# Last layer's output projection as seven-product 2x2 block products, the merged tiles mixed pair by pair

## Chip, core and metric

The kernel runs on one core of one Trainium2 chip. The metric is the time of one execution on the device in microseconds (us), the median over repeated runs. A core has five engines with a queue each that runs in order: TensorE (PE, with its weight loads as PEld), VectorE (DVE), ScalarE (ACT), GpSimd (POOL) and SyncE (SP), which here only issues DMAs. PE's products are added up in PSUM, in tiles of 128x512 float32 (a bank each); DVE and ACT read them from there.

## What is computed

Two residual layers over x of 1024 positions by 1024 channels, float32. The edit touches the end of the second:

```
y_a = (o_a * silu(z_a)) @ w_attn_proj[l]          # 512 -> 1024 channels
y_f = (fourier(u_f) * silu(z_f)) @ w_fourier_proj[l]
m   = sigmoid(g_a + b_a) * y_a + sigmoid(g_f + b_f) * y_f
x   = x + m @ w_out[l]                            # 1024 x 1024 by 1024 x 1024
```

Attention, the Fourier branch, the norms and the input projection stay as they were.

## The kernel before

All activations are kept transposed: 128 channels on the partitions, 1024 positions along the free axis, so 1024 channels are eight tiles t = 0 to 7. A float32 product is made of three faster ones: each operand is split into hi, the value rounded to the shorter type fp32r, and lo, the rest. `mm3` (L162 to L167) adds hi x hi, hi x lo and lo x hi in PSUM, so a 128x128 block by 128x512 costs three matmuls of 128x512. The hi part of a split is a copy and the lo part a subtraction: `split_pool` (L129 to L132) does both on POOL, `split_fast` (L134 to L137) puts the copy on ACT and the subtraction on DVE, `wtile` (L139) loads a weight tile and splits it on POOL. Weight tiles live in the pool `wp`, which has two buffers each of raw, hi and lo. `stage` (L123) loads a 128x1024 tile into one of three buffers.

`merge` (L782) ends a layer. The attention output oG (four tiles) is split. Then for each of eight tiles t: load and sigmoid the gate (L801, L802), load the Fourier term mf, multiply the tile's weights by oG (24 matmuls, PSUM tile ya, two buffers), and on DVE multiply by the gate out of PSUM (L805) and add mf (L806), both 1024 wide; the result sa is the merged tile. It is split into mT, hi on ACT (L807) and lo on DVE (L808). After all eight, the output projection runs eight tiles xo of 8 K-tiles x 2 halves x 3 = 48 matmuls. The first runs its last K-tile last (`fm_late`), since mT's last tile comes late. DVE adds x to each finished xo (L821), and SP stores it (L822), the last tile in two halves. For the first layer, the same loop also feeds the next layer.

Memory pools lie on two sides of SBUF, which the layers swap: in the last layer mT is on the left with `wp` and `stage`, oG on the right; in layer 0 mT is on the right. What an engine does next is not the program's order alone: the tile framework's scheduler plans each queue when the kernel is built, by program order among what it expects to be ready, and adds the waits. At run time each queue then goes strictly in that planned order.

Of the kernel before, what the change touches and what calls it, by code (L numbers as in the profile page):

```python
# [33 lines left out]
F_ATT = (0, 0, 0, 0, 2, 0, 0, 0, 0, 0, 0, 0, 0, 0, 0, 1, 0, 1, 0, 0, 0, 1, 0, 0, 0, 1, 0, 0, 0, 1, 0, 0, 0, 1, 0, 0, 0, 0, 0, 0, 0, 1, 0, 0, 0, 1, 0, 0, 0, 1, 0, 0, 0, 0, 0, 0, 0, 1, 0, 0, 0, 0, 0, 1)  # L34
B_P, B_E, B_PT, B_KT, B_PF, B_S = (6, 8), 4, 4, 2, 2, 3
ORD = "SFVV"
SEQ = ('u z0 T F0 z1 C0 G0 F1 z2 C1 F2 G1 C2 F3 z3 M C3 G2 G3', 'u z0 T F0 z1 C0 G0 F1 z2 C1 F2 G1 C2 F3 z3 G2 M C3 G3')
U0, ZF0, GA0, GF0 = 4, 8, 12, 20


def f(ap):
    return ap.bitcast(F32)


class Trunk:
# [355 lines left out]
    def phase_a(self, l, xg, fp, gF):  # L401
# [330 lines left out]
    def attention(self, l, ap, sum_e):  # L732
# [7 lines left out]
        for i, (h, c) in enumerate(units):  # L740
            nxt = self.prep(l, *units[i + 1], ap, st) if i + 1 < len(units) else None
            for j in range(4):
                k = 2 * j
                for what in ORD:
                    if what == "S" and nxt:
# [33 lines left out]
            cur = nxt  # L779
        return za  # L780

    def merge(self, l, og3, x_ctx, res_d, out_d):  # L782
        tc, nc, io = self.tc, self.nc, self.io
        sub, mult, add = ALU.subtract, ALU.mult, ALU.add
        for _ in self.filler:
            pass
        self.psum(f"pm{l}")
        x_ctx.close()
        xs, os = self.xs, self.os
        m_ctx = ExitStack()  # L790
        mp = m_ctx.enter_context(tc.tile_pool(name=f"m{l}", bufs=1, side=xs))
        with tc.tile_pool(name=f"og{l}", bufs=1, side=os) as op_:
            oG = [op_.tile([P, 4, S], F32R, name=f"oG{j}") for j in range(2)]
            mT = [mp.tile([P, KD, S], F32R, name=f"mT{j}") for j in range(2)]
            for t in range(4):
                o = self.stage(self.og_d[t], f"og{t}") if t < 3 else og3
                nc.scalar.activation(oG[0][:, t, :], o, AF.Copy)
                nc.vector.tensor_tensor(oG[1][:, t, :], o, f(oG[0][:, t, :]), op=sub)
            for t in range(KD):
                sa = op_.tile([P, S], F32, tag="sa", bufs=2, name=f"sa{t}")  # L800
                nc.sync.dma_start(sa, self.ga_d[t])  # L801
                nc.scalar.activation(sa, sa, AF.Sigmoid, bias=self.bm[:, l, 0, t:t + 1])  # L802
                mf = self.stage(self.mf_d[t], f"mfl{t}")
                ps = self.fm(self.wtile(io["w_ap"][l, t], 4, f"wa{t}"), oG, 4, f"ya{t}")
                nc.vector.tensor_tensor(sa, ps, sa, op=mult)  # L805
                nc.vector.tensor_tensor(sa, sa, mf, op=add)  # L806
# [4 lines left out]
        if not last:  # L811
            xp = n_ctx.enter_context(tc.tile_pool(name=f"x{l + 1}", bufs=1, side=os))
            xg = [xp.tile([P, KD, S], F32R, name=f"xg{l + 1}{j}") for j in range(2)]
        with tc.tile_pool(name=f"xo{l}", bufs=1, side=xs) as op_:
            for t in range(KD):
                xr = self.stage(res_d[t], f"xr{t}")
                w = self.wtile(io["w_o"][l, t], KD, f"wo{t}")
                ps = self.fm_late(w, mT, f"xo{t}") if t == 0 else self.fm(w, mT, KD, f"xo{t}")
                dst = out_d[t] if last else self.x1_d[t]
                for cs in (slice(0, 512), slice(512, S)) if last and t == KD - 1 else (slice(0, S),):  # L820
                    nc.vector.tensor_tensor(xr[:, cs], ps[:, cs], xr[:, cs], op=add)  # L821
                    nc.sync.dma_start(dst[:, cs], xr[:, cs])  # L822
                if not last:
                    self.feed(l + 1, t, xr, op_, xg)
            if not last:
                self.norm(op_)
        m_ctx.close()
        return None if last else (xg, n_ctx)

    def run(self):  # L830
        tc, nc, io = self.tc, self.nc, self.io
        x_ctx = ExitStack()
        xp = x_ctx.enter_context(tc.tile_pool(name="x0", bufs=1, side="right"))
        xg = [xp.tile([P, KD, S], F32R, name=f"xg0{j}") for j in range(2)]
        raw = self.wp.tile([P, 1024], F32, tag="raw", name="wu0_r")
# [117 lines left out]
```

## Time and profile before

| what | value |
|---|---|
| median of 3 runs | 1682.37 us (1681.14 to 1683.57) |
| profiled execution | 1685.97 us, of which the span 1684.2 us |
| PE, PEld busy | 1651.1 us (98%), 1348.4 us (80%) |
| DVE, ACT, POOL busy | 833.5 us (49%), 635.8 us (38%), 727.9 us (43%) |
| last merge: ya stage, xo stage | 1547.6 to 1592.4 us, 1592.4 to 1679.5 us |

The span runs from the first to the last instruction of the program; the profiled execution's own time has some 2 us around it. Busy time of an engine is time in which an instruction of it runs; for an engine that waited inside an instruction, for a shared resource, that time counts as busy too. Matmuls overlap in the record, so PE's pace is read from the distance of their starts or from a stretch divided by their number, not from the duration of one (some 390 ns here).

### The profile page before, as it was taken

Reading aid. Unit: us, or ns where it says so; the run is one execution under the profiler, and the core shown is the slowest. Engines: PE = TensorE matmul, PEld = TensorE weight load, DVE = VectorE, ACT = ScalarE, POOL = GpSimd, SP = SyncE. Lnnn points to the kernel's source line nnn. Section 1 sums busy time; section 2 is a strip of 40 time slices with the busy share of each in tenths; the row PEclk is TensorE's granted clock in tenths of the full one; section 3 lists DMA queues with packets and bytes.
Section 4 is the critical chain, followed back from the end, with each engine's and each line's share of the span. In section 5 each row is a group of like instructions: output and inputs, shape, how many; then the busy total and the mean of one; then the engine's idle time right before and its main releaser. Section 6 shows DMA issues by size and latency. Waiting matters only on the chain.

```text
span 1684.2 us, 22506 instructions
## 1 busy us (share of the span) xinstructions
PE 1651.1 (98%) x8374; PEld 1348.4 (80%) x8374; DVE 833.5 (49%) x1358; ACT 635.8 (38%) x1233; POOL 727.9 (43%) x567
## 2 busy tenths in 40 slices
PE   7999999999999999999999999999999999999998
PEld 5888889887777877777888888888877777777887
DVE  7643452332666666565324435424246666664711
ACT  4322321312666666522112223213147666663300
POOL 5622361474453543443254324524643545543531
PEclk9999999999999999999999999999999999999999
DMA  5302230343555553474342023213454555534741
GB/s 193 131 13 70 90 125 32 126 181 131 191 183 184 179 186 143 156 241 158 126 144 75 13 77 115 106 50 129 173 172 165 192 176 188 192 143 163 239 148 76
DMA packets 118366, 234.76 MB, mean 139 GB/s; under 512 B 27888, under 2 KB 48624, under 8 KB 118000
## 3 DMA queue, kind: packets, MB, share of 16 engines
q1 hardware_dynamic: 117904, 228.59, 39.4%
q0 software_dynamic: 352, 4.73, 0.7%
q8 instruction: 66, 1.08, 0.3%
q14 instruction: 44, 0.36, 0.1%
HBM read 116.89 MB, written 49.28 MB: 99 GB/s over the span
## 4 chain that ended last, share of the span: by engine, by line
PE 86%; DMA 4%; DVE 3%; ACT 3%; issue 2%; POOL 1%; SPq 0%; DVEq 0%; ACTq 0%; POOLq 0%
PE pt L714 4%; PE s L165 4%; PE o L718 4%; PE o L720 3%; PE s L167 3%; PE s L166 3%; PE gf L167 3%; PE gf L166 3%; PE gf L165 3%; PE xo L166 3%; PE xo L167 3%; PE xo L165 3%; PE ga L165 3%; PE ga L167 3%; PE ga L166 3%; DMA P<-E 2%
## 5 line engine op out<-in xcount | busy, mean ns | idle before, releaser
L693 DVE TENSOR_REDUCE nm<-s 128x1 f32<-128x512 f32 x256 | 173.0, 687 | 110.4 <-PE s L167 109.0
L700 ACT ACTIVATE E<-s,nm 128x512 f32<-128x512 f32 x256 | 173.3, 684 | 57.5 <-issue 28.6
L714 PEld LDWEIGHTS pt<-identr,P 128*128 128x128 f32 x1024 | 114.4, 141 | 43.0 <-DMA P<-E 7.4
L131 POOL TENSOR_SCALAR pT<-pf 128x512 fp32r<-128x512 f32 x96 | 59.4, 619 | 188.4 <-ACT pf L725 167.6
L132 POOL TENSOR_TENSOR pT<-pf,pT 128x512 fp32r<-128x512 f32 x96 | 123.7, 1289 | 8.0
L714 PE MATMUL pt<-identr,P 128*128 128x128 f32 x1024 | 121.7, 239 | 5.5 <-DMA P<-E 5.5
L196 DVE TENSOR_TENSOR pT<-pt,pT 128x512 fp32r<-128x512 f32 x160 | 109.3, 685 | 28.8 <-ACT pT L195 27.0
L165 PE MATMUL s<-kT,qT 96*128 96x512 f32 x256 | 110.8, 433 | 3.6 <-ACT E L700 2.4
L195 ACT ACTIVATE pT<-pt 128x512 fp32r<-128x512 f32 x160 | 95.7, 598 | 44.5 <-PE pt L714 44.5
L718 PE MATMUL o<-pT,V 128*128 128x512 f32 x256 | 109.7, 429 | 0.0
L720 PE MATMUL o<-pT,V 128*128 128x512 f32 x256 | 106.9, 418 | 0.0
L165 PE MATMUL ga<-xg,wga_h 128*128 128x512 f32 x256 | 103.4, 404 | 0.0
L167 PE MATMUL ga<-xg,wga_l 128*128 128x512 f32 x256 | 102.7, 401 | 0.0
L166 PE MATMUL ga<-xg,wga_h 128*128 128x512 f32 x256 | 102.2, 399 | 0.0
L165 PE MATMUL gf<-xg,wgf_h 128*128 128x512 f32 x256 | 101.0, 395 | 0.0
L166 PE MATMUL s<-kT,qT 96*128 96x512 f32 x256 | 100.9, 394 | 0.0
L167 PE MATMUL gf<-xg,wgf_l 128*128 128x512 f32 x256 | 100.9, 394 | 0.0
L166 PE MATMUL gf<-xg,wgf_h 128*128 128x512 f32 x256 | 100.9, 394 | 0.0
L167 PE MATMUL s<-kT,qT 96*128 96x512 f32 x256 | 97.4, 397 | 0.0
L165 PE MATMUL xo<-mT,wo_h 128*128 128x512 f32 x224 | 87.9, 392 | 0.0
L166 PE MATMUL xo<-mT,wo_h 128*128 128x512 f32 x224 | 87.9, 392 | 0.0
L167 PE MATMUL xo<-mT,wo_l 128*128 128x512 f32 x224 | 87.9, 392 | 0.0
(334 smaller groups left out, 4221.3 us busy)
## 6 DMA issues: line engine op xcount, KB each, us to landing
P<-E SPq DMA_DIRECT2D x256, 256.0 KB, 2.3
kv_d<-KV SPq DMA_DIRECT2D x16, 640.0 KB, 2.9
KVh<-kv_d SPq DMA_DIRECT2D x16, 640.0 KB, 4.6
wgf_r<-in_w_fm SPq DMA_DIRECT2D x16, 512.0 KB, 3.5
mf_d<-sgf SPq DMA_DIRECT2D x16, 512.0 KB, 3.3
wga_r<-in_w_fm SPq DMA_DIRECT2D x16, 512.0 KB, 3.6
ga_d<-sga SPq DMA_DIRECT2D x16, 512.0 KB, 2.7
sa<-ga_d SPq DMA_DIRECT2D x16, 512.0 KB, 3.8
```

The source lines that it names most:

```text
L131: nc.gpsimd.tensor_scalar(hi, src, 1.0, 1.0, op0=ALU.mult, op1=ALU.mult)
L132: nc.gpsimd.tensor_tensor(lo, src, f(hi), op=ALU.subtract)
L165: self.nc.tensor.matmul(out, ah, bh, start=(i == 0), stop=False)
L166: self.nc.tensor.matmul(out, ah, bl, start=False, stop=False)
L167: self.nc.tensor.matmul(out, al, bh, start=False, stop=(i == n - 1))
L195: nc.scalar.activation(hi, ps, AF.Copy)
L196: nc.vector.tensor_tensor(lo, ps, f(hi), op=ALU.subtract)
L693: nc.vector.tensor_reduce(nm2[:, kc:kc + 1], s_ps, axis=AX.X, op=ALU.max)
L700: nc.scalar.activation(e, halves[kc], AF.Exp, bias=nm, accum_out=sum_e[:, h, t, kc:kc + 1])
L714: nc.tensor.transpose(tp[:, j * P:(j + 1) * P].bitcast(F32R), u["P"][j][k // 4][:, (k % 4) * P:(k % 4 + 1) * P], self.identr)
L718: nc.tensor.matmul(u["o"], u["V"][:, kk, :], q[0], start=(u["n"] == 0), stop=False)
L720: nc.tensor.matmul(u["o"], u["V"][:, kk, :], q[1], start=False, stop=(u["n"] == ST))
```

## The change

The first layer keeps `merge`. The last one has a `merge_last` of its own. Its output product is done on blocks: for output tiles 2j and 2j + 1 (j = 0 to 3) the weights are a 2x2 matrix of 128x512 blocks (row = output tile, column = half of the K axis), and the merged activations are a 2x2 matrix of 512x512 blocks B11, B12, B21, B22 (row = half of the channels, column = half of the positions). Seven block products and sums take the place of eight products (the form of Strassen's scheme that shares its sums). The right-hand operands are B11, B21, B22 and four mixtures: T1 = B12 - B11, T3 = B22 - B12, T2 = B22 - T1, T4 = B21 - T2. They are split once into M1 (B11), M2 (B21, B22), XA (T1, T3) and XB (T4, T2). The left-hand operands are weight blocks and four sums S1 to S4 per j, made on POOL in float32 and split block by block on ACT and DVE.

The merged tiles come in the order 0 4 1 5 2 6 3 7, with the weights of a pair (k, k + 4) loaded and split on POOL at once, and the mixtures of K-tile k are made when the pair is done. Of them, two subtractions 512 wide go on POOL after the second tile, one after the first, and one on DVE; XB's lo part is on POOL for k < 2 and on DVE after. The gate tiles sa have four buffers instead of two, on the left side.

`stream` runs the 28 block products as steps (j, i), i being the product: (0, 0), (1, 0), (0, 2), (1, 2), and then the rest by j. A weight operand is prepared two steps ahead (`AHEAD`). PSUM has three pairs of banks: b1 for products 0 and 2, bx for 1, 3 and 5, bz for 4 and 6. A product that shares a bank with an earlier one is added to what stands there, after the earlier state has been read out: by ACT (i = 0) or by DVE. x is added on POOL, three times per j, and once by DVE on the way out of PSUM; stores are 512 wide.

```diff
+AHEAD = 2
+B11, T2, B21, T3, T1, T4, B22 = range(7)
...
+    def merge(self, l, og3, x_ctx, res_d):
...
-        last = l + 1 == L
...
-                dst = out_d[t] if last else self.x1_d[t]
-                for cs in (slice(0, 512), slice(512, S)) if last and t == KD - 1 else (slice(0, S),):
-                    nc.vector.tensor_tensor(xr[:, cs], ps[:, cs], xr[:, cs], op=add)
-                    nc.sync.dma_start(dst[:, cs], xr[:, cs])
...
+    def merge_last(self, l, og3, x_ctx, res_d, out_d):
...
+        self.psum(f"pm{l}")
...
+            M1, M2, XA, XB = [[mp.tile([P, 4, n], F32R, name=f"{name}{j}") for j in range(2)]
+                              for name, n in (("M1", 512), ("M2", S), ("XA", S), ("XB", S))]
+            cut = lambda x, cs: [y[:, :, cs] for y in x]
+            self.X = {B11: M1, B21: cut(M2, lo), B22: cut(M2, hi), T1: cut(XA, lo), T3: cut(XA, hi), T4: cut(XB, lo), T2: cut(XB, hi)}
...
+                def pair(k):
+                    raw = self.wp.tile([P, S], F32, tag="raw", name=f"wa{k}_r")
+                    w = [self.wp.tile([P, S], F32R, tag=n, name=f"wa{k}_{n}") for n in ("hi", "lo")]
+                    for j, cs in enumerate((lo, hi)):
+                        nc.sync.dma_start(raw[:, cs], io["w_ap"][l, k + 4 * j])
+                    self.split_pool(raw, *w)
+                    for j, cs in enumerate((lo, hi)):
+                        W[k + 4 * j] = [x[:, cs].rearrange("p (k m) -> p k m", k=4) for x in w]
+                W = {}
+                pair(0)
+                for t in (0, 4, 1, 5, 2, 6, 3, 7):
+                    k = t % 4
+                    sa = sp.tile([P, S], F32, tag="sa", bufs=4, name=f"sa{t}")
+                    nc.sync.dma_start(sa, self.ga_d[t])
+                    nc.scalar.activation(sa, sa, AF.Sigmoid, bias=self.bm[:, l, 0, t:t + 1])
+                    mf = self.stage(self.mf_d[t], f"mfl{t}")
+                    ps = self.fm(W.pop(t), oG, 4, f"ya{t}")
+                    if t < 3:
+                        pair(t + 1)
+                    if t + 1 == KD:
+                        stream = self.stream(l, res_d, out_d)
+                        next(stream)
+                    nc.vector.tensor_tensor(sa, ps, sa, op=mult)
+                    nc.vector.tensor_tensor(sa, sa, mf, op=add)
+                    mixed[t] = sa
+                    if t < 4:
+                        self.split_fast(sa[:, lo], M1[0][:, k], M1[1][:, k])
+                        nc.gpsimd.tensor_tensor(sa[:, lo], sa[:, hi], sa[:, lo], op=sub)
+                        continue
+                    y = mixed[k]
+                    self.split_fast(sa, M2[0][:, k], M2[1][:, k])
+                    if t + 1 == KD:
+                        self.psum(f"px{l}")
+                        next(stream)
+                        next(stream)
+                    nc.vector.tensor_tensor(y[:, hi], sa[:, hi], y[:, hi], op=sub)
+                    nc.gpsimd.tensor_tensor(sa[:, hi], sa[:, hi], y[:, lo], op=sub)
+                    nc.gpsimd.tensor_tensor(sa[:, lo], sa[:, lo], sa[:, hi], op=sub)
+                    nc.scalar.activation(XB[0][:, k], sa, AF.Copy)
+                    (nc.gpsimd if k < 2 else nc.vector).tensor_tensor(XB[1][:, k], sa, f(XB[0][:, k]), op=sub)
+                    self.split_fast(y, XA[0][:, k], XA[1][:, k])
+            self.cp = ctx.enter_context(tc.tile_pool(name=f"xo{l}", bufs=1, side=os))
+            for _ in stream:
+                pass
+    def stream(self, l, res_d, out_d):
+        nc, io = self.nc, self.io
+        add, sub = ALU.add, ALU.subtract
+        J = KD // 2
+        steps = [(0, 0), (1, 0), (0, 2), (1, 2)]
+        steps += [(j, i) for j in range(J) for i in ((1, 3, 4, 5, 6) if j < 2 else range(7))]
+        loads = [s for s in steps if s[1] < 2]
+        last = {(j, r): max(steps.index((j, i)) for i in ((0, 1, 2) if r == 0 else (1, 5))) for j in range(J) for r in range(2)}
+        R, ops, sums, banks, tiles, xr, pair = {}, {}, {}, {}, {}, {}, {}
+        early, nb = 2, 4
+        def pump(n):
+            while len(R) < (len(loads) if self.cp else early) and (len(R) < early + nb or last[loads[len(R) - nb]] < n):
+                j, i = loads[len(R)]
+                if len(R) < early:
+                    R[j, i] = self.wp.tile([P, S], F32, tag="raw", name=f"wx{j}{i}")
+                else:
+                    R[j, i] = self.cp.tile([P, S], F32, tag="R", bufs=nb, name=f"wx{j}{i}")
+                nc.sync.dma_start(R[j, i], io["w_o"][l, 2 * j + i])
+        def prep(n):
+            if n >= len(steps):
+                return
+            pump(n)
+            j, i = steps[n]
+            half = lambda r, h: R[j, r][:, h * 512:h * 512 + 512]
+            if i == 1:
+                s1, s2, s3, s4 = sums[j] = [self.cp.tile([P, 512], F32, tag=f"s{m}", name=f"S{m}_{j}") for m in range(1, 5)]
+                nc.gpsimd.tensor_tensor(s1, half(1, 0), half(1, 1), op=add)
+                nc.gpsimd.tensor_tensor(s2, s1, half(0, 0), op=sub)
+                nc.gpsimd.tensor_tensor(s3, half(0, 0), half(1, 0), op=sub)
+                nc.gpsimd.tensor_tensor(s4, half(0, 1), s2, op=sub)
+            if i in (0, 2, 5):
+                src = half(i == 5, i != 0)
+            else:
+                src = sums[j][(None, 1, None, 2, 0, None, 3)[i]]
+            if n % 2 == 0:
+                pair[n] = pair[n + 1] = [self.wp.tile([P, S], F32R, tag=t, name=f"A{t}{n}") for t in ("hi", "lo")]
+            cs = slice(n % 2 * 512, n % 2 * 512 + 512)
+            ops[n] = [x[:, cs] for x in pair.pop(n)]
+            self.split_fast(src, *ops[n])
+            pump(n + 1)
+        def store(j, m, x, cs):
+            nc.sync.dma_start(out_d[2 * j + m][:, cs], x[:, cs])
+        def base(x, cs, r):
+            nc.gpsimd.tensor_tensor(x[:, cs], x[:, cs], r[:, cs], op=add)
+        for n in range(AHEAD):
+            prep(n)
+        yield
+        V = nc.vector
+        lo, hi = slice(0, 512), slice(512, S)
+        for n, (j, i) in enumerate(steps):
+            prep(n + AHEAD)
+            tag = ("b1", "bx", "b1", "bx", "bz", "bx", "bz")[i]
+            fresh = i in (0, 1, 4)
+            if fresh:
+                banks[j, tag] = self.ps.tile([P, 512], F32, tag=tag, bufs=2, name=f"{tag}_{j}")
+            b = banks[j, tag]
+            ah, al = ops.pop(n)
+            bh, bl = self.X[i]
+            for k in range(4):
+                ks = slice(k * P, k * P + P)
+                nc.tensor.matmul(b, ah[:, ks], bh[:, k, :], start=(fresh and k == 0), stop=False, skip_group_check=True)
+                nc.tensor.matmul(b, ah[:, ks], bl[:, k, :], start=False, stop=False, skip_group_check=True)
+                nc.tensor.matmul(b, al[:, ks], bh[:, k, :], start=False, stop=(k == 3), skip_group_check=True)
+            if i in (0, 1 if j > 1 else 2):
+                tiles[j, int(i == 0)] = self.sa_p.tile([P, S], F32, tag="sa", bufs=4, name=f"c{j}{int(i == 0)}")
+            for m in range(2):
+                if i == (((2, 1), (0, 2))[j > 1][m]):
+                    xr[j, m] = self.stage(res_d[2 * j + m], f"xr{j}{m}")
+            a, t, ra, rt = tiles.get((j, 0)), tiles[j, 1], xr.get((j, 0)), xr.get((j, 1))
+            if i == 0:
+                nc.scalar.activation(t[:, lo], b, AF.Copy)
+            elif i == 1:
+                V.tensor_tensor(a[:, hi], b, t[:, lo], op=add)
+                base(a, hi, ra)
+            elif i == 2:
+                V.tensor_tensor(a[:, lo], b, ra[:, lo], op=add)
+                store(j, 0, a, lo)
+            elif i == 3:
+                V.tensor_tensor(t[:, hi], b, t[:, lo], op=add)
+            elif i == 4:
+                V.tensor_tensor(t[:, hi], b, t[:, hi], op=add)
+                base(t, hi, rt)
+                store(j, 1, t, hi)
+            elif i == 5:
+                V.tensor_tensor(t[:, lo], b, t[:, lo], op=add)
+                base(t, lo, rt)
+                store(j, 1, t, lo)
+            else:
+                V.tensor_tensor(a[:, hi], b, a[:, hi], op=add)
+                store(j, 0, a, hi)
+            yield
...
-            nxt = self.merge(l, og, x_ctx, res, io["out"])
-            if nxt:
-                xg, x_ctx = nxt
+            if l + 1 < L:
+                xg, x_ctx = self.merge(l, og, x_ctx, res)
+        self.merge_last(l, og, x_ctx, res, io["out"])
```

## Rows read from the trace of the kernel before

**Rows 1.** The page, parts 1 and 2: busy us (share), instructions; granted clock.

```profile
PE 1651.1 (98%) x8374; PEld 1348.4 (80%) x8374; DVE 833.5 (49%) x1358; ACT 635.8 (38%) x1233; POOL 727.9 (43%) x567
...
PEclk9999999999999999999999999999999999999999
```

**Rows 2.** Stretches: us, PE, PEld, DVE, ACT, POOL busy; clock, DMA, GB/s.

```profile
1547.60:1592.43 44.83, 44.35 (x190) 35.41 (x190) 29.06 (x22) 13.61 (x13) 19.88 (x16) 1.00 0.74 240
1592.43:1603.56 11.13, 11.13 (x51) 9.20 (x50) 6.12 (x5) 2.65 (x3) 4.30 (x3) 1.00 0.52 183
1603.56:1679.51 75.95, 75.94 (x336) 62.53 (x334) 8.38 (x7) 0.00 (x0) 20.62 (x12) 1.00 0.31 111
1679.51:1684.20 4.69, 0.00 (x0) 0.00 (x0) 1.29 (x2) 0.00 (x0) 0.00 (x0) 0.76 0.29 112
```

**Rows 3.** Waits from 1545.3 on: waiting group, releaser; total us, times, longest.

```profile
DVE xr L821 <- PE xo L167: 67.6, 7, 9.7
POOL wo_h L131 <- PE xo L166: 36.5, 5, 7.3
...
DVE mT L808 <- ACT mT L807: 9.1, 8, 1.2
...
PE ya L165 <- DVE sga L472: 0.9, 1, 0.9
```

**Rows 4.** The chain from 1592.43 to its end: start us, us, what.

```profile
1592.43 0.23 PE xo L187
...
1679.27 0.24 PE xo L167
...
1679.54 0.69 DVE xr L821
1680.23 0.60 DVEq L947
```

**Rows 5.** A stretch of layer 0's xo, PE alone, columns likewise.

```profile
773.60:850.00 76.40, 76.40 (x329) 1.00 0.37 131
```

**Rows 6.** DVE, then POOL, in order of time: start us, us, instruction.

```profile
1556.16 1.64 DVE L806 TENSOR_TENSOR sa<-sa,mfl 128x1024 f32<-128x1024 f32 x1
...
1561.55 1.22 DVE L806 TENSOR_TENSOR sa<-sa,mfl 128x1024 f32<-128x1024 f32 x1
...
1587.99 1.23 DVE L805 TENSOR_TENSOR sa<-ya,sa 128x1024 f32<-128x1024 f32 x1 [0.58 <-ACT sa L802]
1589.25 2.63 DVE L806 TENSOR_TENSOR sa<-sa,mfl 128x1024 f32<-128x1024 f32 x1
1593.01 1.40 DVE L808 TENSOR_TENSOR mT<-sa,mT 128x1024 fp32r<-128x1024 f32 x1 [1.13 <-ACT mT L807]
...
1588.41 2.40 POOL L132 TENSOR_TENSOR wo_l<-wo_r,wo_h 128x1024 fp32r<-128x1024 f32 x1
1592.29 1.05 POOL L131 TENSOR_SCALAR wo_h<-wo_r 128x1024 fp32r<-128x1024 f32 x1 [1.49 <-PE ya L166]
1593.43 3.25 POOL L132 TENSOR_TENSOR wo_l<-wo_r,wo_h 128x1024 fp32r<-128x1024 f32 x1
```

**Rows 7.** Groups of 128x512 forms: busy us, mean ns, idle before.

```profile
L132 POOL TENSOR_TENSOR pT<-pf,pT 128x512 fp32r<-128x512 f32 x96 | 123.7, 1289 | 8.0
...
L196 DVE TENSOR_TENSOR pT<-pt,pT 128x512 fp32r<-128x512 f32 x160 | 109.3, 685 | 28.8 <-ACT pT L195 27.0
...
L195 ACT ACTIVATE pT<-pt 128x512 fp32r<-128x512 f32 x160 | 95.7, 598 | 44.5 <-PE pt L714 44.5
...
L320 DVE TENSOR_TENSOR fold<-fy,fold 128x512 fp32r<-128x512 f32 x16 | 10.8, 739 | 2.8 <-ACT fold L319 2.8
```

**Rows 8.** DVE, then POOL, ahead of the ya stage.

```profile
1533.73 1.23 DVE L798 TENSOR_TENSOR oG<-za,oG 128x1024 fp32r<-128x1024 f32 x1 [2.49 <-ACT oG L797]
...
1545.82 0.69 DVE L472 TENSOR_TENSOR sga<-ga,rb 128x512 f32<-128x512 f32 x1 [1.69 <-PE ga L167]
...
1545.65 0.62 POOL L131 TENSOR_SCALAR wa_h<-wa_r 128x512 fp32r<-128x512 f32 x1 [8.84 <-PE ga L166]
```

More of the change, by code (lines that the diff above doesn't have):

```diff
@@ L780, in attention @@
         return za
-    def merge(self, l, og3, x_ctx, res_d, out_d):
+    def merge(self, l, og3, x_ctx, res_d):
         tc, nc, io = self.tc, self.nc, self.io
@@ L808, in merge @@
                 nc.vector.tensor_tensor(mT[1][:, t, :], sa, f(mT[0][:, t, :]), op=sub)
-        last = l + 1 == L
         n_ctx = ExitStack()
-        if not last:
-            xp = n_ctx.enter_context(tc.tile_pool(name=f"x{l + 1}", bufs=1, side=os))
-            xg = [xp.tile([P, KD, S], F32R, name=f"xg{l + 1}{j}") for j in range(2)]
+        xp = n_ctx.enter_context(tc.tile_pool(name=f"x{l + 1}", bufs=1, side=os))
+        xg = [xp.tile([P, KD, S], F32R, name=f"xg{l + 1}{j}") for j in range(2)]
         with tc.tile_pool(name=f"xo{l}", bufs=1, side=xs) as op_:
@@ L818, in merge @@
                 ps = self.fm_late(w, mT, f"xo{t}") if t == 0 else self.fm(w, mT, KD, f"xo{t}")
-                dst = out_d[t] if last else self.x1_d[t]
-                for cs in (slice(0, 512), slice(512, S)) if last and t == KD - 1 else (slice(0, S),):
-                    nc.vector.tensor_tensor(xr[:, cs], ps[:, cs], xr[:, cs], op=add)
-                    nc.sync.dma_start(dst[:, cs], xr[:, cs])
[L823 to L826, printed above, removed]
@@ L827, in merge @@
-        m_ctx.close()
-        return None if last else (xg, n_ctx)
+                nc.vector.tensor_tensor(xr, ps, xr, op=add)
+                nc.sync.dma_start(self.x1_d[t], xr)
+                self.feed(l + 1, t, xr, op_, xg)
+            self.norm(op_)
+        m_ctx.close()
+        return xg, n_ctx
+    def merge_last(self, l, og3, x_ctx, res_d, out_d):
+        tc, nc, io = self.tc, self.nc, self.io
+        sub, mult, add = ALU.subtract, ALU.mult, ALU.add
+        lo, hi = slice(0, 512), slice(512, S)
+        for _ in self.filler:
+            pass
+        self.psum(f"pm{l}")
+        x_ctx.close()
+        xs, os = self.xs, self.os
+        with ExitStack() as ctx:
+            mp = ctx.enter_context(tc.tile_pool(name=f"m{l}", bufs=1, side=xs))
+            sp = ctx.enter_context(tc.tile_pool(name=f"sa{l}", bufs=1, side=xs))
+            M1, M2, XA, XB = [[mp.tile([P, 4, n], F32R, name=f"{name}{j}") for j in range(2)]
+                              for name, n in (("M1", 512), ("M2", S), ("XA", S), ("XB", S))]
+            cut = lambda x, cs: [y[:, :, cs] for y in x]
+            self.X = {B11: M1, B21: cut(M2, lo), B22: cut(M2, hi), T1: cut(XA, lo), T3: cut(XA, hi), T4: cut(XB, lo), T2: cut(XB, hi)}
+            self.sa_p, self.cp = sp, None
+            mixed = {}
+            with tc.tile_pool(name=f"og{l}", bufs=1, side=os) as op_:
+                oG = [op_.tile([P, 4, S], F32R, name=f"oG{j}") for j in range(2)]
+                for t in range(4):
+                    o = self.stage(self.og_d[t], f"og{t}") if t < 3 else og3
+                    nc.scalar.activation(oG[0][:, t, :], o, AF.Copy)
+                    nc.vector.tensor_tensor(oG[1][:, t, :], o, f(oG[0][:, t, :]), op=sub)
+                def pair(k):
[41 more added lines that the diff above has]
+            for _ in stream:
+                pass
@@ new lines, in stream @@
+    def stream(self, l, res_d, out_d):
[46 more added lines that the diff above has]
+        V = nc.vector
+        lo, hi = slice(0, 512), slice(512, S)
+        for n, (j, i) in enumerate(steps):
[40 more added lines that the diff above has]
+            yield
```

## The prediction

> **What bounds the kernel now.** I read the page's first two parts, then the stretches of the last merge, then who waits for whom there, the chain, and DVE and POOL side by side. The page shows PE busy 98% of the span, at full granted clock in every slice [rows 1]. The edit touches only the last 137 us, and there PE is the bound: its own time is 44.4 of 44.8 us in the stage of the eight merged tiles (ya) and all of the output stage (xo) [rows 2]. The waits run one way: DVE waits 67.6 us for xo products, POOL 36.5 us for PE to free a weight slot, while PE's longest total wait is 0.9 us, ahead of the first ya [rows 3]. The chain's xo part goes from 1592.43 to 1679.51 without a gap, then a 0.69 us addition on DVE [rows 4], a second (1.29 us for the two [rows 2]), and a store. Its 8 x 48 = 384 matmuls took 87.1 us, 0.2268 us each. The reader should also see how idle the helpers are in the xo stage (DVE 8.4, ACT 0 and POOL 20.6 of 76.0 us) and how much fuller they are in the ya stage (DVE 29.1, POOL 19.9 of 44.8) [rows 2]. The edit empties PE in the first and loads DVE and POOL in the second.
>
> **Part 1, what PE loses.** A product is one 128x512 weight block against a 512x512 block of the merged tile: 4 K-tiles x 3 split terms = 12 matmuls of 128x512, the form of today. Four row pairs x 7 products make 28 x 12 = 336. 48 matmuls go, 48 x 0.2268 = **-10.9 us**. The pitch is not sure: layer 0's xo, the same form with its operands on the other side of SBUF, took 76.4 us for 329 matmuls, two of them cut by the window's edges, or 0.2333 us each [rows 5]. Bounds for 336 matmuls: 0 and +2.2 us. I take 0, since the new operands lie on the side of today's mT.
>
> **Part 2, the end.** Today two half additions stand behind the last matmul, since DVE begins the first only when the whole tile is done [rows 4]. After, one 512-wide addition and one 256 KB store remain: **-0.6 us**. DMA traffic stays nearly as it was: the same loads of w_o, x, gates and w_ap in the same sizes or halves, and 16 output stores of half size. DMAs are busy 31% of the xo stage [rows 2], so I cost them at nothing; only the first load of a weight pair that waits for oG's memory (step 4) comes after ya, with four products, 10.9 us, to cover it.
>
> **Part 3, what is added to DVE and POOL in the ya stage.** Here the sum is decided. The row that matters is the pair of queues around 1588 to 1598 [rows 6]. DVE's addition L806 (both inputs in SBUF) takes 1.22 us alone; begun at 1589.25, while POOL's subtraction ran from 1588.41 to 1590.81, it took 2.63 and ended 1.07 us after it. POOL's next one, 2.40 alone, took 3.25 beside DVE's 1593.01 to 1594.41. DVE's L805, which reads PSUM, took 1.23 us at 1587.99 beside the same POOL work. So two-SBUF-input work of DVE and work of POOL go one after the other, and a blocked one ends about 0.14 us sooner than its own duration after the holder: call that the port.
>
> The Trainium skill, page "SBUF — State Buffer", section "SBUF: two separate sides", calls it an exclusive lock that whichever instruction starts first keeps for its whole length. The rows agree but for the 0.14 us of overlap; by the rule to the letter the port time below would be 6.5 us longer and the forecast 1685.6 us, by the rows 1679.1.
>
> Port work from the first addition (1556.16 us [rows 6]) until T2's last K-tile is split (XB, k = 3), with durations of [rows 6, 7]:
> - DVE: 8 additions x 1.22 = 9.8; M1 lo 4 x 0.69 = 2.8; M2 lo 4 x 1.23 = 4.9; B22 - B12 4 x 0.69 = 2.8; XA lo of three pairs x 1.23 = 3.7; XB lo of two x 1.23 = 2.5; the A-block splits of steps 0 to 3, 4 x 0.69 = 2.8. Sum 29.3.
> - POOL: weight splits of pairs 2 and 3, 2 x (1.05 + 2.40) = 6.9; three subtractions a pair, 12 x 1.29 = 15.5; XB lo of two pairs x 2.40 = 4.8. Sum 27.2.
>
> That is 56.5 us in 47 pieces; with 46 handovers of 0.14 us, 50.1. The first weight sums of the second matrix (2 x 1.15 net) fall into the same time: 52.4. The 512-wide forms with both inputs in SBUF are read from L320 (0.74 us, contended at times) and from PSUM readers (0.69), so within 0.05 each. The stretch from 1556.16 to the old end of ya at 1592.43 is 36.3 us long: the port is oversubscribed, where today 8 x (1.22 + 1.23) = 19.6 us of DVE and 19.9 of POOL, waits included, share 44.8 [rows 2]. The port also idles, while DVE waits for an ACT half (9.1 us in 8 today [rows 3]) and POOL for DVE: 4 us over the four pairs, which I got by laying both queues side by side by hand, DVE and POOL taking turns. T2 is complete at 1556.2 + 52.4 + 4 = 1612.6.
>
> What can PE do until then? The rest of ya to 1592.43, and after it steps 0 to 3 (48 matmuls on B11 and B21) and k = 0 to 2 of step 4 (9): 57 x 0.2268 = 12.9 us, to 1605.4. It waits **+7.2 us**, whether in ya (DVE reads a finished ya late, and the two-buffer PSUM stops the next tile), before M1's last K-tile, or at step 4. The least is 0.9 us (no idle port, no sums: 1606.3), the most 18 us (nothing gained at handovers, 10 us of idle port, 1625.3, less 2.0 for nine matmuls of step (0, 4) that may be pulled forward). The cover that goes: today DVE's read of a ya tile hides behind the next tile's 24 matmuls, 44.8 / 8 = 5.6 us [rows 2].
>
> **Part 4, the 28 steps.** Port work is 28 splits x 0.69 + 16 sums x 1.29 + 12 residual additions x 1.29 = 55.4 us beside 76.2 us of PE: it fits. ACT gets 32 pieces of 0.60, 19 us [rows 7]. But 16 steps write on in a bank (b1, bx, bz) which DVE or ACT must first have read; one other product, 2.72 us, covers that. The read costs 0.69 us [rows 7]; a split queued ahead of it may wait 1.29 for POOL and run 0.69: 2.67 together, just the cover. Bounds per return 0 and 0.8 us (one more POOL piece ahead, less the slack), 0 to 12.8 us in all. I take 1 us, near the lower end, since order on the queues follows readiness: in today's rows DVE split one og at 1533.73, ahead of a ga result that is older in the program and came at 1545.82 [rows 8]. The sums S1 and S2 come in time where R is loaded, four buffers ahead.
>
> **Start of the stage.** Splitting two w_ap tiles at once (3.45 instead of 1.91 us) is hidden for pair 0: POOL sat idle 8.84 us before 1545.65 [rows 8]. Pair 1 may delay the last og split by 0.7 us, with 36 matmuls on the other K-tiles in hand. Cost 0, bounds -0.5 and +0.7.
>
> **Sum.** -10.9 - 0.6 + 7.2 + 1.0 = -3.3 on the profiled execution's 1685.97 us, of which 1684.2 are its span and 1.8 lie around it: 1682.7. That execution is 3.6 us above the median of the runs, 1682.37, so on the runs' scale: 1682.4 - 3.3 = **1679.1 us**.
>
> **Rivals.**
> 1. *The port hides it.* If the planner pulls XA and XB early and other steps forward, the wait shrinks to 0 to 2.5 us: -11.5 to -8, about 1672. For it: DVE and POOL together still have idle time in the xo stage, and 0.14 us per handover. Against: 52 us of port work do not fit into 36 us, and what can move behind is little, as the mixtures feed four of the seven products.
> 2. *Slower: the bank returns.* Sixteen times a step waits for DVE's or ACT's read of its bank, blocked behind a split that waits for POOL. At 0.8 us each, +12.8 instead of +1.0: 1682.4 - 11.5 + 7.2 + 12.8 = 1690.9. It decides from 0.3 us per return (4.3 us in all: no gain left). For it: a 1.29 us POOL piece is there 28 times. Against: 2.72 us of cover.
> 3. *It does not do what it says on PE.* The products run at layer 0's 0.2333 us because part of M, XA or XB lies elsewhere: +2.2 us, 1681.1.
>
> **Chances.** Forecast (wait of 4 to 10 us) 0.55, spread 1676 to 1682; rival 1 0.20; rival 2 0.17; rival 3 0.08. The range 1672 to 1689 holds the forecast, rival 3, most of rival 1, the bound of 18 us but for 1 us, and the lower part of rival 2. Within 0.2% (3.4 us, about what a measurement of this kernel can tell from no change) means 1679.0 to 1685.7. Faster: 0.20 + half of the forecast = 0.47. Same: the other half and rival 3, 0.36. Slower: 0.17.
>
> **What would show it.** PE: 336 xo matmuls at 0.227 us. Part 3 right: gaps of PE in the ya stage released by DVE's read of ya, then ahead of steps 2 to 4 released by DVE or POOL on M, XA, XB; POOL pieces of 1.29 us lasting over 2. Wrong: no PE gap over 2 us between 1555 and 1615 (rival 1), or regular gaps of 0.5 us and more at every second or third product to the end (rival 2). Part 2: 4.1 us instead of 4.7 [rows 2] behind the last matmul. The forecast falls if the port's work in ya is hidden, or if T2 is late by more than 14 us.

## The result, and the profile after

The changed kernel took 1699.97 us (1698.76 to 1701.02, four runs) beside 1682.97 us for the kernel before on the same chip: a ratio of 1.0097, 95% interval 1.0085 to 1.0110. It is slower by 17 us, where 3.3 us faster was forecast. Its profiled execution took 1701.02 us with a span of 1699.2. The page, parts 1 and 2 (answering [rows 1]):

```profile
PE 1646.4 (97%) x8326; PEld 1341.7 (79%) x8326; DVE 877.9 (52%) x1411; ACT 660.0 (39%) x1273; POOL 761.2 (45%) x585
...
PEclk9999999999999999999999999999999999999899
```

48 matmuls fewer, as the edit says, but PE now loses time at the end. The stretches answer [rows 2] (stretch: us; busy time and instructions of PE, PEld, DVE, ACT, POOL; granted clock, DMA share, GB/s). They are: from the last ga product to the first ya product; the ya stage; to where PE's last gap and its slow matmuls lie behind; the rest of the products; the tail; then two pieces of the ya stage:

```profile
1543.65:1549.20 5.55, 0.39 (x2) 0.03 (x1) 3.86 (x3) 2.64 (x3) 3.39 (x2) 0.85 0.11 46
1549.20:1601.99 52.79, 49.43 (x192) 38.52 (x192) 36.01 (x28) 16.20 (x18) 27.03 (x14) 0.92 0.52 179
1601.99:1633.00 31.01, 18.47 (x64) 14.46 (x64) 19.58 (x20) 9.07 (x13) 17.48 (x11) 0.78 0.32 120
1633.00:1694.50 61.50, 61.50 (x272) 50.42 (x271) 31.94 (x41) 12.66 (x22) 31.22 (x22) 1.00 0.32 111
1694.50:1699.20 4.70, 1.04 (x5) 0.54 (x3) 0.69 (x1) 0.00 (x0) 0.42 (x1) 0.84 0.29 112
...
1549.20:1554.35 5.15, 5.15 (x12) 4.09 (x13) 1.85 (x2) 1.06 (x1) 0.00 (x0) 0.50 0.93 305
1554.35:1579.40 25.05, 25.05 (x109) 20.05 (x108) 16.91 (x13) 5.38 (x6) 12.87 (x7) 1.00 0.43 147
```

The reader should see that from 1633 on PE has no gap and no slow matmul. All the loss lies in the 89 us before, of two kinds: PE stands still, and behind each of four stands its matmuls take 0.43 us instead of 0.227 (5.15 us for 12, at a granted clock of 0.50) before the clock is back at 1.00. The waits of the stretch (group, releaser: total us, times, longest) answer [rows 3]:

```profile
ACT XB L890 <- POOL sa L889: 20.1, 4, 5.8
...
PE b L962 <- DVE sa L874: 9.2, 1, 9.2
...
PE ya L167 <- DVE sga L474: 5.2, 1, 5.2
...
PE ya L167 <- DVE sa L874: 3.4, 3, 2.6
PE b L962 <- ACT c L972: 3.3, 1, 3.3
```

PE waits in four places. In the order of time: 5.2 us ahead of the first ya tile, for DVE's last read of ga; 3.4 us in ya, for DVE's reads of finished ya tiles (L874); 9.2 us ahead of the first product, for the read of the last ya tile, since the products' PSUM pool opens only then; 3.3 us ahead of step (1, 2), for ACT's read of its bank (L972). None of the four is a wait for T2 itself: its split ended at 1625.95, and the first product that reads it began at 1629.68.

Why these reads are late stands in the queues (start us, us, instruction, and in brackets the idle time before it and its releaser). First DVE, POOL and ACT ahead of the first product:

```profile
1601.77 2.12 POOL L888 TENSOR_TENSOR sa<-sa,sa 128x512 f32<-128x512 f32 x1 [5.31 <-DVE M L139]
1602.68 1.22 DVE L874 TENSOR_TENSOR sa<-ya,sa 128x1024 f32<-128x1024 f32 x1
1603.96 1.26 POOL L889 TENSOR_TENSOR sa<-sa 128x512 f32<-128x512 f32 x1
1605.26 1.06 ACT L890 ACTIVATE XB<-sa 128x1024 fp32r<-128x1024 f32 x1 [3.94 <-POOL sa L889]
1606.35 1.23 DVE L891 TENSOR_TENSOR XB<-sa,XB 128x1024 fp32r<-128x1024 f32 x1 [2.45 <-ACT XB L890]
1607.49 1.22 DVE L875 TENSOR_TENSOR sa<-sa,mfl 128x1024 f32<-128x1024 f32 x1
1608.74 0.63 ACT L138 ACTIVATE M<-sa 128x512 fp32r<-128x512 f32 x1 [2.43 <-DVE sa L875]
...
1609.40 0.69 DVE L139 TENSOR_TENSOR M<-sa,M 128x512 fp32r<-128x512 f32 x1 [0.70 <-ACT M L138]
1610.01 1.22 DVE L874 TENSOR_TENSOR sa<-ya,sa 128x1024 f32<-128x1024 f32 x1
...
1618.87 2.16 POOL L928 TENSOR_TENSOR S<-wx,S 128x512 f32<-128x512 f32 x1
1620.99 1.28 POOL L888 TENSOR_TENSOR sa<-sa,sa 128x512 f32<-128x512 f32 x1
1622.34 1.26 POOL L889 TENSOR_TENSOR sa<-sa 128x512 f32<-128x512 f32 x1
1623.64 1.06 ACT L890 ACTIVATE XB<-sa 128x1024 fp32r<-128x1024 f32 x1 [5.57 <-POOL sa L889]
1624.60 0.58 ACT L972 ACTIVATE c<-b 128x512 f32<-128x512 f32 x1
```

A mixture goes POOL, POOL, ACT, DVE, and each engine stands still for it in the middle of its queue. DVE waits 2.45 us for XB of pair 2, and behind that wait stand the addition of ya3, the split of M1 and the read of the last ya tile at 1610.01; that read is what PE waits for from 1601.99 on. Further on, POOL does four weight sums ahead of the mixtures of pair 3; ACT waits 5.57 us for them, and the 0.58 us read of a product's bank stands behind. XB of pair 3, the last K-tile of T2, is split on DVE from 1624.73 to 1625.95.

Behind that, products 1 and 3 of a row pair use the same bank one after the other, and yet PE does not stop between them, because the planner put four matmuls of product 4 there (bz). They cover DVE's read of product 1:

```profile
1632.41 0.39 PE L962 MATMUL bz<-XA,Ahi 128*128 128x512 f32 x1
...
1633.36 0.50 PE L962 MATMUL bx<-XA,Ahi 128*128 128x512 f32 x1
```

At the end there is, as forecast, one addition instead of the two of [rows 2]:

```profile
1695.32 0.24 PE bz L964
...
1695.65 0.69 DVE c L990
```

### The profile page after: what moved, and what is told of

The parts are those of the page before. It is cut to its first block, busy times and chain, and to the rows that moved or that the text cites. A ratio compares the mean times of both kernels' runs of the same rounds, so it can differ in the third digit from the quotient of the medians.

```text
span 1699.2 us, 22555 instructions
## 1 busy us (share of the span) xinstructions
PE 1646.4 (97%) x8326; PEld 1341.7 (79%) x8326; DVE 877.9 (52%) x1411; ACT 660.0 (39%) x1273; POOL 761.2 (45%) x585
## 3 DMA queue, kind: packets, MB, share of 16 engines
q8 instruction: 66, 1.08, 0.3%
## 4 chain that ended last, share of the span: by engine, by line
PE 81%; DMA 5%; DVE 4%; ACT 3%; issue 3%; POOL 3%; SPq 0%; ACTq 0%; POOLq 0%; DVEq 0%
PE pt L716 4%; PE s L167 4%; PE o L720 4%; PE o L722 3%; PE s L169 3%; PE s L168 3%; PE gf L169 3%; PE gf L168 3%; PE gf L167 3%; PE ga L167 3%; PE ga L169 3%; PE ga L168 3%; DMA P<-E 3%; PE aa L167 2%; PE aa L168 2%
## 5 line engine op out<-in xcount | busy, mean ns | idle before, releaser
L727 ACT ACTIVATE pf<-pt 128x512 f32<-128x512 f32 x96 | 57.4, 598 | 75.5 <-PE pt L716 73.9
L500 PE MATMUL c<-wc_h,xg 128*128 128x256 f32 (+1 forms) x256 | 73.6, 290 | 0.7 <-ACT wc_h L160 0.5
L501 PE MATMUL c<-wc_l,xg 128*128 128x256 f32 (+1 forms) x256 | 73.5, 288 | 0.3 <-DVE wc_l L161 0.3
```

The lines of the kernel that those rows point to most:

```text
L500: nc.tensor.matmul(ps, xg[0][:, k, ts], wh[:, k, :], start=(k == 0), stop=False)
```

## The experiments

All twelve are edits of the changed kernel. "From ga to the end" runs from the start of the last ga matmul to the end of the last product: 134.1 us before, 151.9 after. It leaves out the attention stage, where the kernels differ by up to 6.4 us in when the last ga matmul starts (1545.40 before, 1543.65 after; the extremes are 1540.94 in e11 and 1547.36 in e4).

**Mixtures left out** (e1_no_mix): the six lines that form and split XA and XB go, with the first subtraction (L879), and T1 to T4 point at M2's halves, so the output lacks the mixtures.

> Leaves out the four mixtures and their splits (one DVE and three POOL subtractions and two splits per pair; products 1, 3, 4 and 5 read B21 and B22 instead). All 28 steps, sums, banks and both queues' other work stay. Theory A (the mixtures in the ya stage hold up DVE, ACT and POOL, and all PE gaps after the first come from them): the gaps inside ya (4.6 us), most of the 9.4 us ahead of step 0 and the 3.5 us ahead of step 3 go, with some 5 us of slow matmuls behind them: 1680 to 1685 us, about the time of the kernel before. Rival (the 28 steps with their bank returns and sums cost it): no more than 5 us less, 1695 or above.

1680.53 us beside 1683.40, ratio 0.9987 (0.9978 to 0.9996); 133.8 us from ga to the end. The theory held: the mixtures and their splits cost some 19 us, more than the whole loss. Even without them the kernel gains 2.9 us, not 11: PE waits 4.8 us in ya for ACT's half of oG, which comes late.

**No second PSUM pool** (e2_one_psum).

```diff
-                        self.psum(f"px{l}")
...
-  banks[j, tag] = self.ps.tile([P, 512], F32, tag=tag, bufs=2, ...)
+  banks[j, tag] = self.ps.tile([P, 512], F32, tag=tag, bufs=2 if tag == "b1" else 1, ...)
```

> No change of PSUM pool ahead of step 0: b1 keeps two banks, bx and bz one each, beside the four of ya. Theory (step 0 waits for DVE's read of the last ya tile only because the new pool takes over its banks): 18 matmuls of steps 0 and 1 run at about 1602 us on K-tiles 0 to 2, the 9.4 us gap falls to about 4, and steps 2 to 4 move up until the last mixture binds: 3 to 6 us less than the changed kernel, 1694 to 1697. Rival (M1's last K-tile or the mixtures are what it waits for): under 1 us.

1699.15 us, ratio 1.0098 (1.0084 to 1.0111). The wait ahead of the first product is gone, and PE waits for M and XB instead:

```profile
PE b L961 <- ACT M L138: 4.1, 1, 4.1
PE bx L961 <- ACT XB L889: 2.0, 1, 2.0
```

So the rival held: the pool's change only names the place. PE had done 58 matmuls of the products by the time T2 was split (1626.46 us), where the changed kernel had done 39 (1625.95 us), and yet the end came only 0.8 us sooner. What binds is when M, XA and XB are done.

**Gates behind og on ACT** (e3_og_first): `with tc.issue_after(og_last.ins):` around the sigmoids.

> The gates' sigmoids are queued on ACT behind the split of the attention output; nothing else changes. Theory (the fourth gate load, which four buffers let start early, stands at the head of ACT's queue at 1543, and behind it the first split of the attention output, DVE's read of ga and PE): the first gap falls from 5.3 to about 1 us and the slow matmuls behind it go, 5 to 7 us less, 1693 to 1695. Rival (the og loads themselves arrive late, or the later stage gives it back): under 2 us.

1701.45 us, ratio 1.0114 (1.0097 to 1.0131); the wait for ga's last read stays at 5.2 us. ACT's order is not its cause.

**PE kept busy** (e4_keep_busy): 40 matmuls into a spare bank ahead of the last ya tile's read.

> Forty matmuls on a spare bank stand between the last ya tile and step 0 and fill the 9.4 us gap there (40 x 0.2268 = 9.1 us); their result is not used. Theory (after a gap of some us the granted clock is the lower level for 4 to 5 us, so that 11 matmuls take 0.427 instead of 0.227 us): the first matmuls of step 0 run at 0.227 us, 2 to 2.5 us less, 1697.5 to 1698. Rival (they are slow because their operands arrive late): 0, and the 0.427 stays.

1705.70 us, ratio 1.0139 (1.0121 to 1.0157). Behind the spare matmuls the first product runs at full clock:

```profile
1615.55:1618.50 2.95, 2.95 (x13) 2.46 (x14) 2.95 (x4) 1.06 (x1) 1.15 (x2) 1.00 0.91 337
```

That the slow matmuls come from standing still is shown. The time was not gained: a wait of 8.1 us for ACT's bank read came in place of the later one of 3.3, from ga to the end took 155.5 us, and in this kernel ga ended 3.7 us later than in the changed one.

**One weight tile at a time** (e5_single_w): `pair` goes, and each ya tile calls `wtile` as before the change.

> The w_ap tiles are loaded and split one at a time again, each by wtile ahead of its product, as in the kernel before; all else as changed. Theory (the pairwise split, 3.5 instead of 1.9 us on POOL, delays SP's loads of the attention output and holds the port against its split, and DVE's last read of ga and PE wait behind that): the first gap falls from 5.3 to 1 to 2 us and its slow matmuls go, the whole tail moves up by 4 to 6 us: 1694 to 1696. Rival (four gate loads at the start are what delays it): the gap stays above 4 us and the time within 2 us of the changed kernel's 1700.

1698.41 us beside 1684.0, ratio 1.0079 (1.0065 to 1.0093). Neither expectation held in full: the first wait falls from 5.2 to 3.7 us, not to 1 or 2, and PE now waits 4.5 us for weights in ya.

**Mixtures on DVE** (e6_mix_on_dve).

```diff
-                        nc.gpsimd.tensor_tensor(sa[:, lo], sa[:, hi], sa[:, lo], op=sub)
+                        nc.vector.tensor_tensor(sa[:, lo], sa[:, hi], sa[:, lo], op=sub)
...   (the two subtractions and XB's remainder of pairs 0 and 1 likewise)
```

> The three mixture subtractions of each pair and XB's lo part for k < 2 run on DVE instead of POOL (12 x 0.69 instead of 12 x 1.29 us, 2 x 1.22 instead of 2 x 2.40); the same work, 9.6 us less port time. Theory (one port for both engines sets when the last mixture is ready): the last XB split ends 8 to 10 us earlier counted from the first merged tile, and the time falls by 6 to 9 us, 1691 to 1694. Rival (DVE is the bound by its own queue, POOL's help was worth its 15.5 + 4.8 us): slower than the changed kernel, by up to 10 us.

1690.77 us, ratio 1.0037 (1.0025 to 1.0049), 9 us better for the same arithmetic. The theory held. XB of pair 3 begins 8.6 us earlier (DVE):

```profile
1616.12 1.23 DVE L891 TENSOR_TENSOR XB<-sa,XB 128x1024 fp32r<-128x1024 f32 x1
```

The port model gives the size: 12 subtractions at 0.69 instead of 1.29 us and two remainders at 1.23 instead of 2.40 [rows 6, 7] are 9.5 us less port time. Laid side by side, DVE's pieces with both inputs in SBUF and POOL's fill 58.1 of 65.7 us from the first addition to XB's end in the changed kernel, and 49.1 of 56.1 here: 9.0 us less. The edit also makes each chain of mixtures shorter by itself, with fewer changes of engine; that the port alone is worth the 9 us is therefore argued from the sizes, not shown apart.

**Plain products first** (e7_plain_first): B11 and B21 of all four row pairs, eight steps, ahead of the first product with a mixture; the output tiles and weight buffers are laid out anew for that order.

> Order of the steps alone: products 0 and 2 of all four row pairs first (eight steps, 21.8 us, that need only B11 and B21), then 1, 3, 4, 5, 6 of each. Theory (PE waits in the xo stage only for the mixtures): 10.9 us more work stands ahead of the first use of T2, but PE reaches it late anyway, at 1630 against 1626 us, since it also waits for the last ya tile to be read; so it gains 2 to 4 us, mostly the 3.5 us gap and its slow matmuls: 1696 to 1698. Rival (the order does not matter, what waits is the last ya read and M2): within 1 us of the changed kernel.

1698.25 us, ratio 1.0079 (1.0064 to 1.0093). 2 us, just outside the expected range: PE has more to do once it may start, but it still waits 9.4 us for the last ya read.

**The three together** (e8_all_three).

> The three edits of the other kernels of this call together: single w_ap tiles, mixtures on DVE, products 0 and 2 first. Theory (port time and its consequences are all of the loss): the last mixture is ready before the 21.8 us of plain products are done, PE's gaps total under 5 us, and the time is 1674 to 1680 us, below the kernel before. Rival (DVE's longer queue delays its reads of ya, PE stops in ya and the clock drops): 1683 or above.

1693.12 us, ratio 1.0046 (1.0031 to 1.0062), no better than e6 alone, as the rival said. Waits of 5.4 us ahead of the first product and 3.0 us in ya stay, both for DVE's reads of ya (L861 there). So the order on DVE was left to try.

**og's loads first on SP** (e9_og_loads_first).

```diff
+                        with tc.issue_after(og_in.ins) if k else ExitStack():
                             nc.sync.dma_start(raw[:, cs], io["w_ap"][l, k + 4 * j])
...
+                    with tc.issue_after(og_in.ins) if k else ExitStack():
                         nc.sync.dma_start(sa, self.ga_d[t])
```

> The changed kernel with one order changed on SP's queue: the second weight pair of the ya stage and the gate tiles from the third on are loaded behind the three loads of og. Theory (the 5.3 us that PE stands still between the last ga product and the first ya product comes from og landing late, behind half a megabyte of weights and two gate tiles that are not needed yet; ACT then halves og late, DVE's remainder of og stands ahead of its last read of ga): the gap falls to 1 to 2 us and the slow matmuls behind it go, so the median is 3 to 5 us below the changed kernel's, 1695 to 1697 us. Rival (the mixtures decide the end by themselves, so the start is given back at the wait ahead of the first product): the gap falls, the wait ahead of the first product grows by as much, 1699 to 1700 us. Second rival (POOL's split of the second weight pair holds the port against DVE's remainder of og, whatever the loads): the gap stays above 4 us.

1696.74 us beside 1684.95, ratio 1.0070 (1.0054 to 1.0087); from ga to the end 146.8. The theory held. In the changed kernel SP's queue, one of its waits, and what came of it were (SPq is a DMA issue):

```profile
SPq L855 <- POOL wa_lo L134: 2.4, 1, 2.4
...
1536.63 0.81 SPq L855 DMA_DIRECT2D wa_r<-in_w_ap  x2
1537.49 0.43 SPq L865 DMA_DIRECT2D sa<-ga_d  x1
1538.02 1.53 SPq L128 DMA_DIRECT2D og<-og_d  x2
...
1544.25 1.06 ACT L848 ACTIVATE oG<-og 128x1024 fp32r<-128x1024 f32 x1
...
1545.03 2.34 POOL L134 TENSOR_TENSOR wa_lo<-wa_r,wa_hi 128x1024 fp32r<-128x1024 f32 x1
...
1545.34 3.11 DVE L849 TENSOR_TENSOR oG<-og,oG 128x1024 fp32r<-128x1024 f32 x1 [6.01 <-ACT oG L848]
1548.38 0.68 DVE L474 TENSOR_TENSOR sga<-ga,rb 128x512 f32<-128x512 f32 x1
```

and in this run

```profile
1533.60 6.71 SPq L850 DMA_DIRECT2D og<-og_d  x3
...
1543.33 0.69 DVE L474 TENSOR_TENSOR sga<-ga,rb 128x512 f32<-128x512 f32 x1 [3.37 <-PE ga L169]
```

The load of the second weight pair waits for its buffer until POOL's split ends (1534.19 + 2.42 = 1536.61), and og's loads stand behind it on SP. So og is halved late, DVE's remainder of og stands ahead of the last ga read and waits for POOL's split on the port: 3.11 instead of 1.23 us. With og first the wait is 0.9 us, as before the change, and the wait ahead of the first product (9.3 us) did not grow; those in ya grew from 3.4 to 4.6 us. The edit also puts the second pair's split behind the ga read, so it does not separate the late load from the port; by the line above the port's share is 1.9 us.

**All of it, mixtures one tile later** (e10_all_early): e6, e7 and e9, the mixtures of a pair written behind the next pair's first tile, one PSUM pool.

```diff
+                    def mix(y=y, sa=sa, k=k):
...
+                    late.append(mix)
...   (in the next pair, behind its first tile's split)
+                        while late:
+                            late.pop()()
```

> The changed kernel with four edits: og's loads first as in the run beside this one; the mixtures wholly on DVE, those of a pair written behind the next pair's first tile; one PSUM pool for the whole stage (the products take the banks of ya, product by product, without a change of pools); and all eight plain products, 96 matmuls or 21.8 us, ahead of the first product with a mixture. Theory (the loss was never the amount of work but that DVE's reads of ya and the split of merged tiles stood behind mixtures, and that PE had too little else to do until the mixtures were done): PE's gaps shrink to at most 4 us in all between the last ga product and the last matmul, against 25 in the changed kernel; from ga to the end 124 to 128 us against 134.1 before the change, a median of 1672 to 1678 us, faster than both kernels. Rival (DVE now carries about 54 us of work within the 66 us that ya and the plain products take, beside 10 us of POOL's weight splits on the same port, so its reads of ya are late all the same): gaps of 8 to 12 us remain, 1682 to 1688 us.

1696.31 us, ratio 1.0067 (1.0054 to 1.0080); 146.0 us. Neither held. The waits ahead of the first product with a mixture shrank as the theory said, but ten new ones (4, 4, 1 and 1 times) came behind 1624 us, all released by DVE's reads of a product (c and t), beside one of 0.5 us for a weight block. The edit had put bx and bz of a row pair into two halves of one tile, and a write to one half waited for the read of the other too. So product 4 waited for the read of product 3 (L994), and its matmuls no longer stood ahead of product 3, which now waited for the read of product 1 (L991):

```profile
PE bx L974 <- DVE c L991: 4.0, 4, 1.4
PE bx L974 <- DVE t L994: 3.5, 4, 0.9
PE bx L974 <- DVE t L1000: 0.9, 1, 0.9
PE bx L974 <- DVE t L996: 0.9, 1, 0.9
PE ya L167 <- DVE sa L879: 2.8, 1, 2.8
PE b L976 <- DVE Alo L139: 2.6, 1, 2.6
```

This is the prediction's rival 2, made by an edit: a return costs 0.9 us where no other product can stand between.

**bx and bz in banks of their own again** (e11_banks): as e10, but each product that opens a bank (0, 1 and 4) takes one of four; 3 and 5 still write on in product 1's, 6 in product 4's.

```diff
+                banks[j, tag] = self.ps.tile([P, 512], F32, tag="b1", bufs=4, name=f"{tag}_{j}")
```

> As the run with all four edits, but each product opens a bank of its own, of four, instead of one half of a two-bank tile. Theory (that run's eleven gaps of 0.93 to 1.77 us behind 1624 us, 11.5 us idle and some 3 us of slow matmuls behind them, are bank returns: a product that writes where the last product's result has not been read yet, here even in the other half of its tile): they go, from ga to the end 131 to 133 us against 134.1 before the change, 1680 to 1684 us, a ratio to before of 0.997 to 1.000. Rival (DVE is too full for the reads to come in time, whichever bank it is): gaps of 0.5 us and more stay behind 1624 us at every second product, 1688 to 1694 us.

1679.24 us beside 1683.28, ratio 0.9980 (0.9971 to 0.9989); 132.1 us. The theory held: no wait is left behind 1624 us, and the four matmuls of product 4 stand ahead of product 3 again. This kernel is faster than both, by 0.2% against the kernel before. In the profiled executions 2.0 us of that lie between ga and the end; ga itself ended 4.5 us earlier, and nothing here shows that an edit is the cause.

**Last mixtures behind four more products** (e12_banks_late).

```diff
+            for _ in range(4):
+                next(stream)
+            late.pop()()
```

> As e11 with the mixtures of the last pair written behind four more plain products, whose weight blocks DVE and ACT then split first. Theory (the 2.96 and 0.69 us gaps at 1604 to 1612 us, released by DVE's splits of M and of a weight block, come from the last mixtures standing ahead of those splits): PE's gaps from ga to the end are at most 5 us in all, 127 to 130 us from ga to the end, 1676 to 1680 us, a ratio of 0.995 to 0.998. Rival (the mixtures are now late for the first product that reads them, at 1616 us): a gap of 2 to 6 us ahead of it takes back what the splits gave, as in e11.

1679.21 us, ratio 0.9974 (0.9963 to 0.9986); 130.2 us. The theory held. PE's waits, all of them, and its stretches (ya; plain products; the rest):

```profile
PE ya L167 <- DVE sa L879: 3.0, 1, 3.0
PE ya L167 <- DVE sga L474: 0.9, 1, 0.9
PE b L975 <- ACT t L983: 0.7, 1, 0.7
PE b L976 <- DVE M L139: 0.3, 1, 0.3
```

```profile
1543.94:1593.57 49.63, 46.66 (x192) 37.20 (x193) 42.83 (x40) 19.66 (x21) 11.24 (x6) 0.97 0.62 222
1593.57:1617.00 23.43, 22.41 (x95) 17.09 (x94) 22.02 (x24) 10.59 (x16) 8.50 (x5) 1.00 0.42 148
1617.00:1672.60 55.60, 55.60 (x244) 45.02 (x242) 30.27 (x38) 10.42 (x18) 33.63 (x24) 1.00 0.36 128
```

The trace shows the wait of 2.6 us for a weight block's split gone against e11; the times of the two don't tell them apart. DVE is now busy 42.83 of 49.63 us in ya and 22.02 of 23.43 after it: that cover is used up, and the 3.0 us wait that is left comes from a split of XA that waited for POOL's last weight split (DVE 3.42 us from 1568.19, POOL 2.72 us from 1567.81). Which of e10's edits, kept here, won how much was not tried one by one.

## Why the prediction was wrong

The step that failed is Part 3's "It waits +7.2 us", with its neighbour "Start of the stage ... Cost 0". The mechanism, the port of DVE and POOL, is borne out by the traces; its size and the form in which PE pays for it were wrong. From trace to trace (us):

| term | forecast | measured |
|---|---|---|
| Part 1, 48 matmuls | -10.9 | -10.9 |
| Part 3, waits in ya and ahead of the products | +7.2 | +12.6 |
| Part 4, bank returns | +1.0 | +3.5, in one place |
| start of the stage | 0 | +4.3 |
| slow matmuls behind the waits | not in the sum | +7.7 |
| Part 2, tail | -0.6 | -1.0 |
| when ga ends (stage before) | not in the sum | -1.75 |
| sum | -3.3 | +14.45; profiled executions +15.05 |

Waits are counted as the distance of two matmul starts less 0.227, less what the kernel before had there (1.0 at the start, 0.7 in ya); slow matmuls as what 37 distances of 0.39 to 0.56 us have above 0.227. Some 0.6 us remain in smaller pieces.

- *Part 3.* T2 was complete at 1625.95, not 1612.6: 4.15 us because the first addition began at 1560.31 instead of 1556.16, which is the start's own wait and the slow matmuls behind it, less the earlier ga; 5.7 because 58.1 us of port work stood ahead instead of 52.4 (3.8 for two more weight sums and the last XA, which the planned order put first, and 1.9 because overlap took off only 4.8 us, not 6.7); 3.5 because the port idled 7.5 us instead of 4. That is near the upper bound of the text, 1625.3, which was made up of other shares.
- *What PE could do meanwhile.* The forecast let 57 matmuls run ahead of T2; the changed kernel did 39. The forecast took for granted that a read of ya and a split of M wait for the port only. They stand in the queues behind mixtures that wait for another engine, so PE stood still 9.2 us where, without the change of pools (e2), it went on with the first product at once. Of the signs that the text named, waits for DVE's read of ya and POOL pieces of over 2 us (2.12, 2.16) came; a wait for M, XA or XB ahead of steps 2 to 4 did not. e12 shows the reverse: the same work, with the mixtures on DVE and behind these reads and with more products ahead of them, costs PE 4 us.
- *Start.* "Pair 1 may delay the last og split by 0.7 us" looked at POOL and at the split alone. The two loads of pair 1 were moved ahead of og's loads on SP, and wait there (e9): a queue that the text did not look at for this step.
- *The clock.* No term stood for it. The longest wait in the stretch before was 0.9 us [rows 3]; the forecast itself put 7.2 us of waiting into one stretch and did not ask what PE's clock does behind it.
- *Part 4 and rivals 2 and 3.* From 1633 on PE has no gap, and 272 recorded matmuls took 61.50 us: no bank returns at each step, and not layer 0's pitch of 0.2333. The one return that cost 3.3 us is ACT's read behind XB. So the kernel is slower for a reason that rival 2 did not name. The text's cover of one other product is not there in its own order of steps for product 3, which follows product 1 in the same bank where j is 0 or 1; the planner's four matmuls of product 4 made up for it, and that was luck as far as the text goes. Its bound of 0.8 us a return does not follow from its terms either: 1.29 us less the 0.05 between 2.72 and 2.67 is 1.24, and e10 measured 0.9. Rival 3's time should read 1681.3, not 1681.1.
- *Rival 1* fell in the changed kernel. e12 goes part of the way to its 1672: 1679.2, where the port is hidden but for 4 us. That this is also the forecast's 1679.1 is chance: it is another kernel.

What stays open: why the stage before ga ends up to 6.4 us earlier or later from kernel to kernel was not tried. In the profiled executions e12 is 7.3 us ahead of the kernel before, of which 3.9 lie between ga and the end (134.1 less 130.2), 2.7 before and 0.7 behind; the lead of 4.1 us in the medians (1679.21 beside 1683.28) cannot be divided so.

## What to carry to other kernels

Cost a new helper chain not by its sum of durations alone: write down, on each in-order queue that it passes, which older reads stand behind its waits, and who waits for those reads. Work for DVE and POOL with both inputs in SBUF adds up on one port, so put it on the engine that does it faster, here DVE. Where PE is taken from full work to waits of several microseconds, add slow matmuls behind each wait to the sum, as a possible cost of its own.

## What the runs showed of the hardware

- In the changed kernel the granted clock fell to 0.50 (5.15 us of the ya stage above; this is the level of 1.2 GHz) behind the waits of 5.2, 2.6, 9.2 and 3.3 us, for 7 to 12 matmuls each. The length of a wait alone does not decide it: in e11 it was 1.00 behind a wait of 2.6 us ahead of a product (1609.90 to 1615.00), and in e9 it was 0.50 behind one of 1.7 us in ya (1575.17 to 1578.16). The repeated waits of up to 1.4 us behind 1625 us in e10 left it at 1.00, as its stretch shows:

```profile
1625.43:1689.83 64.40, 55.47 (x228) 41.53 (x228) 27.43 (x34) 9.23 (x16) 31.46 (x22) 1.00 0.29 98
```

The Trainium skill, page "TensorE: Matmul & The Clock Gate", section "Back-to-back issue gap", has formulas for the gap of a single matmul by itself; worked out for 512 columns, an estimate, they give 426.7 ns at the lower level, and the trace agrees (5.15 us for 12, 429 ns). At the upper level the estimate by its formula is 215.8 ns; here 61.50 us for 272 are 226 ns, and the measurement decides.
- The port's rule, one engine after the other, held outside ya too: DVE's remainder of og, begun at 1545.34 beside POOL's split of 1545.03 to 1547.37, ended at 1548.45, 1.08 us after it; in [rows 6] it was 1.07.
